# Gates, branch projections and feed forward computed token-major instead of channel-major

## The chip, the cores and the metric

The kernel runs on one core of one Trainium2 chip, in one launch. The metric is device time in microseconds, the median of several runs. Engines are named as the profile names them: PE (TensorE matmul), PEld (its weight load), DVE (VectorE), ACT (ScalarE), POOL (GpSimd), SP (which issues DMAs here).

## The reference

Two blocks, each two layers deep, run on `x` of 256 tokens by 1024 channels in float32. The first block is a mixer of three groups of 512 channels (block attention, HGRN2, memory attention); the second has a mixer (delta rule, retention, pooling) and a SwiGLU feed forward of 2816 hidden channels. What the change touches:

```
# first block, per layer; z has 3 x 512 channels
y = jnp.concatenate([o_a, o_h, o_m], axis=-1) * jax.nn.silu(z)
x = x + y @ w_out[l]

# second block, mixer, per layer; gates have 3 x 1024 channels
o_dn  = (rms-normalised o_dn) * dn_out_norm * jax.nn.silu(dn_z)
o_ret = (normalised o_ret) * ret_out_norm * jax.nn.silu(ret_g)
gt = jax.nn.sigmoid(gates).reshape(b, s, N_BRANCH, D_MODEL)
y = (gt[:, :, 0] * (o_dn @ w_branch_dn) + gt[:, :, 1] * (o_pool @ w_branch_pool)
     + gt[:, :, 2] * (o_ret @ w_branch_ret))
return y @ w_out

def swiglu(h, w_gate, w_up, w_down):
    return (jax.nn.silu(h @ w_gate) * (h @ w_up)) @ w_down
```

## The kernel before

**Products in three parts.** A float32 product is made of three matmuls on rounded operands: high by high, high by low, low by high. Activations lie transposed (channels on partitions) in `aTh` and `aTl`, 512 channels by 256 tokens each. Weights come as units of 256 x 512 numbers (512 KB): a DMA into `raw` (three buffers), a cast on ACT to the high part `wh`, a subtraction on DVE to the low part `wl`. Class `Stream` (L224) does this ahead of use, with six slots for split units and two spare ones for some of them; a slot is free when the last matmul of its unit has been issued. SP's queue issues the loads in the order of use.

**Two ways to run a projection.** `tok` (L545) is token-major: for each of the two tiles of 128 tokens, the activations are the stationary operand and 512 weight columns move; the result `acc` has tokens on partitions. It takes a unit in the first token tile and frees it in the second. `chan` (L566) is channel-major: 128 weight columns are stationary and the 256 tokens move; the result has channels on partitions, which is the layout that a next contraction wants. With four column blocks it takes its units in a first pass over two blocks and frees them in a second; in the feed forward (two blocks) it takes and frees a unit at once.

**Where each is used.** Channel-major before: f and q of the first block (`hgrn_f`, L826), the three z (L850), k, q and v of the delta branch with their convolution (L1568), `dn_z` and `ret_g` (L1588), the six gates (L1594), the six branch products (L1599), and gate and up of the feed forward from its third tile of 256 hidden channels on (L1681). Token-major: the other projections, and the first 512 hidden channels. `gated` (L632) turns a branch's output with four 128 x 128 transposes on PE (`to_T`, L425) and multiplies by the silu of z. `ffn` (L1658) does the down projection of tile j - 2 after gate and up of tile j; `hid` holds the hidden channels as high and low parts `ff`.

**What sets the order.** Work is written as generators that yield what they wait for. `Order` (L146) keeps an estimate of PE's time and of when each tile is ready, and after every few matmuls (`poll`) it issues the steps whose inputs it takes to be ready within 200 ns. So the place of a transpose in PE's queue follows from an estimate; on the chip each engine takes its queue in order and waits for its inputs by semaphores. PSUM has three `acc` banks and five `mx` banks; in the feed forward four `mx` banks hold the down projection's sums.

Of the kernel before, what the change touches and what calls it, by code (L numbers as in the profile page):

```python
# [20 lines left out]
NT = 2  # L21
# [5 lines left out]
NJ = D_FF // 256  # L27
NEG = -1.0e30
# [7 lines left out]
SKEW, FSKEW, URGENT = 3, 3, 4  # L36
# [187 lines left out]
class Stream:  # L224
# [15 lines left out]
    def _dma(self):  # L240
        i = self.n_dma
        ap = self.units[i][1]
        _, kk, n = ap.shape
        t = self.kb.p_raw.tile([P, 1024], F32, tag="raw", name=f"raw{i}")
        self.kb.nc.sync.dma_start(t[:, : kk * n].rearrange("p (k n) -> p k n", k=kk), ap)
# [3 lines left out]
        self.n_dma += 1  # L249

# [7 lines left out]
    def _split_h(self):  # L258
# [10 lines left out]
        w = math.prod(self.units[i][1].shape[1:])  # L269
# [3 lines left out]
    def _split_l(self):  # L273
        i = self.n_l
        w = math.prod(self.units[i][1].shape[1:])
# [17 lines left out]
    def take(self, key):  # L293
# [11 lines left out]
        _, kk, n = self.units[i][1].shape  # L305
# [13 lines left out]
def rows(ap, r0, c0, kk, n):  # L319

    return ap[r0 : r0 + kk * P, c0 : c0 + n].rearrange("(k p) n -> p k n", p=P)


class Kernel:
# [92 lines left out]

    def copy(self, dst, src):
# [38 lines left out]
    def silu(self, out, x, gain=None):  # L457

        yield x
        zc, s = self.k2([P, 2, S], "zc"), self.k2([P, 2, S], "sg")  # L460
# [3 lines left out]
        if gain is None:  # L464
            self.dve.tensor_tensor(out, zc, s, op=ALU.mult)
        else:
            for j in range(2):
                self.dve.scalar_tensor_tensor(out[:, j, :], zc[:, j, :], gain[j], s[:, j, :], op0=ALU.mult, op1=ALU.mult)
# [5 lines left out]
    def halves(self, x):  # L474
        return [x[:, 512 * i : 512 * i + 512] for i in range(2)]
# [69 lines left out]
    def tok(self, hT, keys, evac, own=True):  # L545


        w = {}
        for t in range(NT):
            if own:  # L550
                self.join_hT(t)
            for key in keys:
                ps = self.acc()
                for u in range(KD // 2):
                    if t == 0:
                        w[key, u] = self.stream.take((key, u))
                    for k in range(2):
                        kk = 2 * u + k
                        self.mm3(ps, tuple(x[:, kk % 4, t * P : (t + 1) * P] for x in hT[kk // 4]),
                                 tuple(x[:, k, :] for x in w[key, u]), kk == 0, kk == KD - 1)  # L560
# [5 lines left out]
    def chan(self, hT, key, evac, nu=KD // 2, ku=2, nj=4, own=True):  # L566

        if own:
            self.join_hT(0, 1)
# [62 lines left out]
    def gated(self, o, sz, oT, t, needs):  # L632

        yield needs
        ts = slice(t * P, (t + 1) * P)
        on = o()
        yield on
        tp = self.to_T(on)
        yield [tp] + list(sz)
        y = self.k2([P, 4, P], "y")  # L640
        for j in range(2):
            self.dve.tensor_tensor(y[:, 2 * j : 2 * j + 2, :], tp[:, 2 * j : 2 * j + 2, :], sz[j][:, :, ts], op=ALU.mult)
        yield y
        d = (slice(None), slice(None), ts)
        yield from self.split(oT[0][d], oT[1][d], y)
        yield oT[1]
# [166 lines left out]
    def layer1(self, l, hT, mem, nxt):  # L813
# [33 lines left out]
        for br in (1, 0, 2):  # L847
            gain = [ogain[:, 0:1]] * 2 if br == 1 else None
            sz = [self.k2([P, 2, S], "sz") for _ in range(2)]
            self.chan(hT, (l, f"z{br}"), lambda j, ps: self.silu(sz[j], ps, gain))  # L850
            oT[br] = self.part()
            for t in range(NT):
                o.spawn(self.gated(lambda key=(br, t): on[key], sz, oT[br], t, [f"on{l}{br}{t}"]), f"oT{l}{br}{t}")
# [273 lines left out]
    def units2(self, l):  # L1127
# [22 lines left out]
        for n in ("gate", "up"):  # L1150
            cols("f" + n, a[f"ffn_{n}_2"][l], 0, spare=True)

        def down(j, i, spare):
            u.append((((l, "fdown", j), i), rows(a["ffn_down_2"][l], 256 * j, 512 * i, 2, 512), spare))

        for j in range(2, NJ):
            for n in ("gate", "up"):
                for i in range(2):
                    u.append((((l, "f" + n, j), i), rows(a[f"ffn_{n}_2"][l], 512 * i, 256 * j, 4, 256), False))
            if j - 2 < NJ - FSKEW:  # L1160
                for i in range(2):
                    down(j - 2, i, False)
        for j, i in self.last_downs():
            down(j, i, True)
        return u

    def last_downs(self):
        return [(j, i) for i in range(2) for j in range(NJ - FSKEW, NJ - 1)] + [(NJ - 1, i) for i in range(2)]
# [35 lines left out]
    def retention(self, l, qT, kT, rv, on):  # L1204
# [15 lines left out]
        yield [f"rv{l}0", f"rv{l}1"]  # L1220
        yield [R0, R1, rv]
        for t in range(NT):
# [6 lines left out]
            self.o.spawn(self.ret_norm(t, ps, on), f"on{l}ret{t}")  # L1229

    def ret_norm(self, t, ps, on):
# [9 lines left out]
        dve.tensor_tensor(o, o, self.bc(r), op=ALU.mult)  # L1241
# [287 lines left out]
    def gate_evac(self, sg, ps):  # L1529
        yield ps  # L1530
        z = self.k2([P, 2, S], "gz")
# [3 lines left out]
    def branch_evac(self, br, c, j, ps, sg, y, yT):  # L1535
# [7 lines left out]
        if br == "dn":  # L1543
            d = (slice(None), slice(2 * j, 2 * j + 2), slice(None))
            yield y
            yield from self.split(yT[c][0][d], yT[c][1][d], y)
            yield yT[c][1]

    def mixer2(self, l, hT, nxt):
# [6 lines left out]
        self.load(lay[:, 52:56], a["ret_out_norm_2"][l].rearrange("(n p) -> p n", p=P))  # L1556
# [29 lines left out]
        for br, n, gain in (("dn", "dn_z", [lay[:, 48:49]] * 4), ("ret", "ret_g", [lay[:, 52 + j : 53 + j] for j in range(4)])):  # L1586
            sz[br] = [self.k2([P, 2, S], "sz") for _ in range(2)]
            self.chan(hT, (l, n), lambda j, ps: self.silu(sz[br][j], ps, gain[2 * j : 2 * j + 2]))  # L1588
        y = [[self.k2([P, 2, S], "y") for _ in range(2)] for _ in range(2)]
        yT = []  # L1590

        def gate(br, c):
            sig = [self.k2([P, 2, S], "sig") for _ in range(2)]
            self.chan(hT, (l, ("g", br, c)), lambda j, ps: self.gate_evac(sig[j], ps))  # L1594
            return sig

        def branch(br, c, sig):
            o.join(*([f"oT{l}pool"] if br == "pool" else [f"oT{l}{br}{t}" for t in range(NT)]))
            self.chan([oT[br]], (l, ("b", br, c)),  # L1599
                      lambda j, ps: self.named(f"y{l}{br}{c}{j}", self.branch_evac(br, c, j, ps, sig[j], y[c][j], yT)),  # L1600
                      nu=2, own=False)

        for br, _ in self.B2_GATES:
            if br != "pool":
                oT[br] = self.part()
                for t in range(NT):
                    o.spawn(self.gated(lambda key=(br, t): on[key], sz[br], oT[br], t, [f"on{l}{br}{t}"]), f"oT{l}{br}{t}")
# [10 lines left out]
        for c in range(2):  # L1618
            for j in range(2):
                for t in range(NT):  # L1620
                    o.spawn(self.named_wait(f"y{l}dn{c}{j}"), f"yT{l}{c}{j}{t}")
        self.out_proj([(yT[p], (l, "wo2", p), [f"yT{l}{p}0", f"yT{l}{p}1"]) for p in range(2)], SKEW,
# [10 lines left out]
    def ff_first(self, gate, key, t, ps, f, hid):  # L1633

        if gate:
            yield from self.silu(f.rearrange("p (a b) -> p a b", a=2), ps.rearrange("p (a b) -> p a b", a=2))
            return
# [3 lines left out]
        tp = self.to_T(f)  # L1641
        ts = slice(t * P, (t + 1) * P)
        yield tp
        for j in range(2):
            self.act.copy(hid[j][:, 0, :, ts], tp[:, 2 * j : 2 * j + 2, :])
        for j in range(2):
            yield hid[j]
            self.dve.tensor_tensor(hid[j][:, 1, :, ts], tp[:, 2 * j : 2 * j + 2, :], hid[j][:, 0, :, ts].bitcast(F32), op=ALU.subtract)
        yield hid[1]

    def ff_up(self, ps, f, hid):
        yield [ps, f]
        self.dve.tensor_tensor(f, ps, f, op=ALU.mult)
        yield f
        yield from self.split(hid[:, 0], hid[:, 1], f)
        yield hid

    def ffn(self, l, hT, nxt):  # L1658
        a, o = self.a, self.o
        hid = {j: self.k4([P, 2, 2, S], "ff", F32R) for j in range(2)}  # L1660
        f1 = [self.k2([P, 512], "f") for t in range(NT)]
        self.tok(hT, [(l, "fgate"), (l, "fup")],
                 lambda key, t, ps: self.named(f"ff{l}{key[1]}{t}", self.ff_first(key[1] == "fgate", key, t, ps, f1[t], hid)))
# [4 lines left out]
        def down(j, t, i):  # L1668
            o.join(*([f"ff{l}fup{t}" for t in range(NT)] if j < 2 else [f"ff{l}{j}"]))
# [8 lines left out]
        for j in range(2, NJ):  # L1678
            f = self.k2([P, 2, S], "f")
            hid[j] = self.k4([P, 2, 2, S], "ff", F32R)  # L1680
            self.chan(hT, (l, "fgate", j), lambda _, ps: self.silu(f, ps), nu=2, ku=4, nj=2)  # L1681
            self.chan(hT, (l, "fup", j), lambda _, ps: self.named(f"ff{l}{j}", self.ff_up(ps, f, hid[j])), nu=2, ku=4, nj=2)
            if j - 2 < NJ - FSKEW:
                for t in range(NT):
                    for i in range(2):
                        down(j - 2, t, i)
# [117 lines left out]
```

## Time and profile before

| what | value |
|---|---|
| median of 3 runs | 1437.85 us (1437.79 to 1439.17) |
| profiled execution | 1441.07 us, span 1439.3 us |
| mean granted TensorE clock | 0.996 |
| PE busy | 1403.6 us (98%), 9772 matmuls |
| DVE busy | 1024.6 us (71%) |
| ACT busy | 831.5 us (58%) |
| read from HBM | 228.76 MB |

The span runs from the first to the last instruction of the profiled execution; its time also has what lies around them. Matmuls are pipelined, so the records of one and the next overlap, and a busy PE is not one at its peak: how far apart matmuls begin tells more than how long each lasts.

### The profile page before, as it was taken

To read this page: it belongs to the slowest core of one execution; us is meant where nothing else is said; L and a number is where in the kernel's file an instruction comes from. 1 tells how busy PE (TensorE), PEld (TensorE's weight loads), DVE (VectorE), ACT (ScalarE), POOL (GpSimd) and SP (SyncE) were. 2 spreads that over 40 slices of the span, in tenths; PEclk is the share of its full clock that TensorE was granted. 3 is DMA by queue.
4 is the path that set the end of the run, shared out by engine and by line. 5 is a ranking of instruction groups with operands and counts; after the bars stand their busy time and mean duration, and the time that the engine had idled before them with its cause. 6 is when DMAs were issued, how large, how long until landed. Compare 5 with 4: busy or idle time off the path is not lost.

```text
span 1439.3 us, 24675 instructions
## 1 busy us (share of the span) xinstructions
PE 1403.6 (98%) x9772; PEld 1285.8 (89%) x9772; DVE 1024.6 (71%) x1684; ACT 831.5 (58%) x1396; POOL 24.0 (2%) x65
## 2 busy tenths in 40 slices
PE   6899999999998999999999999999999999999998
PEld 6778998888997899999988999979899999799997
DVE  5887778598777698585677656687976577765554
ACT  5875666586665476554655545556655456554553
POOL 6000000000000000000000000000000000000000
PEclk9999999999999999999999999999999999999999
DMA  8752455554256464253475666645543355566662
GB/s 273 173 163 75 132 206 177 185 164 118 60 188 228 126 186 126 90 162 97 156 235 166 186 188 189 215 136 156 153 135 109 105 154 204 184 190 190 184 183 88
DMA packets 156564, 231.41 MB, mean 161 GB/s; under 512 B 27168, under 2 KB 65696, under 8 KB 156448
## 3 DMA queue, kind: packets, MB, share of 16 engines
q1 hardware_dynamic: 156416, 229.84, 52.5%
q8 instruction: 76, 1.25, 0.4%
q14 instruction: 40, 0.33, 0.1%
q0 software_dynamic: 32, 0.00, 0.0%
HBM read 228.76 MB, written 1.05 MB: 160 GB/s over the span
## 4 chain that ended last, share of the span: by engine, by line
PE 76%; DMA 9%; DVE 8%; ACT 4%; issue 2%; SPq 0%; DVEq 0%; ACTq 0%
PE acc L134 53%; PE mx L134 19%; DVE wl L108 4%; PE mx L142 4%; DMA raw<-in_w_in 3%; DMA raw<-in_w_out 3%; ACT wh L108 3%; DMA raw<-in_ffn_up 1%; DMA raw<-in_w_mem_kv 1%; DVE aTl L108 1%; DMA raw<-in_ffn_down 0%; DVE x L108 0%; DMA gain<-in_norm_g 0%; ACT hE L108 0%; ACT junk L108 0%
## 5 line engine op out<-in xcount | busy, mean ns | idle before, releaser
L108 DVE TENSOR_TENSOR wl<-raw,wh 128x1024 fp32r<-128x1024 f32 x412 | 502.2, 1223 | 209.7 <-ACT wh L108 205.9
L108 ACT CAST wh<-raw 128x1024 fp32r<-128x1024 f32 x412 | 429.6, 1048 | 317.7 <-PE acc L134 148.7
L134 PE MATMUL acc<-aTh,wh 128*128 128x256 f32 x1792 | 514.1, 287 | 0.0
L134 PE MATMUL acc<-aTh,wl 128*128 128x256 f32 x1792 | 508.3, 284 | 0.6 <-DVE wl L108 0.6
L134 PE MATMUL acc<-aTl,wh 128*128 128x256 f32 x1792 | 507.6, 283 | 0.0
L134 PEld LDWEIGHTS acc<-aTh,wl 128*128 128x128 f32 x1792 | 343.5, 192 | 2.4 <-DVE wl L108 0.8
L134 PEld LDWEIGHTS acc<-aTh,wh 128*128 128x128 f32 x1792 | 343.4, 192 | 1.9 <-issue 0.5
L134 PEld LDWEIGHTS acc<-aTl,wh 128*128 128x128 f32 x1792 | 343.3, 192 | 0.0
L134 PE MATMUL acc<-wh,aTh 128*128 128x512 f32 x496 | 201.0, 406 | 6.0 <-ACT aTh L108 4.7
L134 PE MATMUL acc<-wh,aTl 128*128 128x512 f32 x496 | 195.4, 395 | 0.8 <-DVE aTl L108 0.8
L134 PE MATMUL acc<-wl,aTh 128*128 128x512 f32 x496 | 195.8, 395 | 0.0
L134 PEld LDWEIGHTS acc<-wh,aTh 128*128 128x128 f32 x496 | 94.4, 190 | 26.3 <-ACT aTh L108 5.8
L134 PEld LDWEIGHTS acc<-wh,aTl 128*128 128x128 f32 x496 | 93.9, 189 | 21.9 <-DVE aTl L108 2.3
L134 PE MATMUL mx<-wh,ff 128*128 128x512 f32 x352 | 111.6, 390 | 0.0
L134 PEld LDWEIGHTS acc<-wl,aTh 128*128 128x128 f32 x496 | 94.2, 190 | 18.4 <-issue 0.5
L134 PEld LDWEIGHTS mx<-wh,ff 128*128 128x128 f32 x352 | 66.2, 188 | 13.4
L108 ACT ACTIVATE sg<-sg 128x512 f32<-128x512 f32 x116 | 73.1, 630 | 1.9
L134 PE MATMUL mx<-wl,ff 128*128 128x512 f32 x176 | 68.7, 390 | 0.0
L108 ACT ACTIVATE sg<-zc 128x512 f32<-128x512 f32 x58 | 36.5, 628 | 22.8 <-DVE zc L108 22.8
L108 ACT ACTIVATE sig<-gz 128x512 f32<-128x512 f32 x24 | 15.2, 632 | 57.8 <-DVE gz L108 57.8
L134 PEld LDWEIGHTS mx<-wl,ff 128*128 128x128 f32 x176 | 33.1, 188 | 6.2
L108 DVE TENSOR_SCALAR zc<-acc 128x512 f32<-128x512 f32 x46 | 31.6, 686 | 9.5 <-PE acc L134 9.5
(311 smaller groups left out, 1593.0 us busy)
## 6 DMA issues: line engine op xcount, KB each, us to landing
raw<-in_w_in SPq DMA_DIRECT2D x200, 512.0 KB, 4.2
raw<-in_ffn_gate SPq DMA_DIRECT2D x44, 512.0 KB, 3.9
raw<-in_ffn_up SPq DMA_DIRECT2D x44, 512.0 KB, 4.6
raw<-in_ffn_down SPq DMA_DIRECT2D x44, 512.0 KB, 4.2
raw<-in_w_out SPq DMA_DIRECT2D x40, 512.0 KB, 3.8
raw<-in_w_mem_kv SPq DMA_DIRECT2D x16, 512.0 KB, 4.2
raw<-in_w_branch_pool SPq DMA_DIRECT2D x8, 512.0 KB, 3.7
raw<-in_w_branch_ret SPq DMA_DIRECT2D x8, 512.0 KB, 4.5
```

What stands on the lines that cost most here:

```text
L108: r = f(out, *args, **kw)
L134: self._ns.matmul(out, lhsT, rhs, **kw)
L142: self._ns.transpose(out, x, ident)
```

## The change

All the projections named above as channel-major, except f, q and the delta branch's k, q and v, go through `tok`. Their results have tokens on partitions. `turn` is new: it transposes a token-major product and splits it into the high and low parts; a gain per channel is applied there. It serves `gated` (which now multiplies first and turns the product) and the delta branch's sum `y` ahead of the output projection. In the feed forward gate and up run by chunks of 512 hidden channels (a last one has 256 columns of either in one unit, `flast`), and each chunk's product is turned with four transposes per token tile; the down projection of chunk c - 1 follows gate and up of chunk c. The gain of the retention's norm varies along the free axis now and is loaded as a broadcast tile. `cols`, `rows` and `Stream` are adapted to units that come from two loads.

```
+    def turn(self, x, oT, t, gain=None):
+        yield x
+        d = (slice(None), slice(None), slice(t * P, (t + 1) * P))
+        tp = self.to_T(x)
+        yield tp
+        if gain is None:
+            self.act.copy(oT[0][d], tp)
+        else:
+            self.act.activation(oT[0][d], tp, AF.Copy, scale=gain)
+        yield oT[0]
+        if gain is None:
+            self.dve.tensor_tensor(oT[1][d], tp, oT[0][d].bitcast(F32), op=ALU.subtract)
...
     def gated(...)
-        tp = self.to_T(on)
-        yield [tp] + list(sz)
-        y = self.k2([P, 4, P], "y")
-        for j in range(2):
-            self.dve.tensor_tensor(y[:, 2 * j : 2 * j + 2, :], tp[:, 2 * j : 2 * j + 2, :], sz[j][:, :, ts], op=ALU.mult)
-        yield y
-        yield from self.split(oT[0][d], oT[1][d], y)
+        yield [on, sz[t]]
+        y = self.k2([P, G], "y")
+        self.dve.tensor_tensor(y, on, sz[t], op=ALU.mult)
+        yield from self.turn(y, oT, t, gain)
...
-            self.chan(hT, (l, f"z{br}"), lambda j, ps: self.silu(sz[j], ps, gain))
+            self.tok(hT, [(l, f"z{br}")], lambda key, t, ps: self.silu(sz[t], ps))
...
     def units2(...)
+        for c in range(NC):
+            cols(("fgate", c), wg, 512 * c, spare=c == 0)
+            cols(("fup", c), wu, 512 * c, spare=c == 0)
+            if c:
+                down(c - 1)
...
     def ret_norm(...)
-        dve.tensor_tensor(o, o, self.bc(r), op=ALU.mult)
+        for h in range(4):
+            dve.scalar_tensor_tensor(o[:, h, :], o[:, h, :], r[:, h : h + 1], gain[:, h * P : (h + 1) * P],
+                                     op0=ALU.mult, op1=ALU.mult)
...
     def branch_evac(...)
         if br == "dn":
-            yield from self.split(yT[c][0][d], yT[c][1][d], y)
+            yield from self.turn(y, yT[c], t)
...
     def mixer2(...)
-            self.chan(hT, (l, n), lambda j, ps: self.silu(sz[br][j], ps, gain[2 * j : 2 * j + 2]))
+            self.tok(hT, [(l, n)], lambda key, t, ps: self.silu(sz[br][t], ps))
...
-            self.chan(hT, (l, ("g", br, c)), lambda j, ps: self.gate_evac(sig[j], ps))
+            self.tok(hT, [(l, ("g", br, c))], lambda key, t, ps: self.gate_evac(sig[t], ps))
...
-            self.chan([oT[br]], (l, ("b", br, c)),
+            self.tok([oT[br]], [(l, ("b", br, c))],
...
     def ff_up(...)
         self.dve.tensor_tensor(f, ps, f, op=ALU.mult)
         yield f
-        yield from self.split(hid[:, 0], hid[:, 1], f)
+        n = 2 * len(hid)
+        tp = self.to_T(f, n)
+        yield tp
+        for j, x in enumerate(hid):
+            self.act.copy(x[:, 0, :, ts], tp[:, 2 * j : 2 * j + 2, :])
+        for j, x in enumerate(hid):
+            yield x
+            self.dve.tensor_tensor(x[:, 1, :, ts], tp[:, 2 * j : 2 * j + 2, :], x[:, 0, :, ts].bitcast(F32), op=ALU.subtract)
...
     def ffn(...)
-        for j in range(2, NJ):
-            self.chan(hT, (l, "fgate", j), lambda _, ps: self.silu(f, ps), nu=2, ku=4, nj=2)
-            self.chan(hT, (l, "fup", j), lambda _, ps: self.named(f"ff{l}{j}", self.ff_up(ps, f, hid[j])), nu=2, ku=4, nj=2)
+        for c in range(NC + 1):
+            keys = [(l, (n, c)) for n in (("fgate", "fup") if c < NC else ("flast",))]
+            for ks in ([keys] if c == 0 else [[k] for k in keys]):
+                self.tok(hT, ks, evac)
```

On PE, in the feed forward of the second block's first layer, the end of an up projection and the start of the down projection behind it, before. `acc` is the up projection's sum, `mx` with `ff` the down projection's.

```order
L134 MATMUL acc_9038<-aTh_8416,wl_8928 128x256
L134 MATMUL acc_9038<-aTl_8417,wh_8927 128x256
L134 MATMUL mx_8780<-wh_8954,ff_8522 128x512
L134 MATMUL mx_8780<-wl_8955,ff_8522 128x512
L134 MATMUL mx_8780<-wh_8954,ff_8522 128x512 x2
L134 MATMUL mx_8780<-wl_8955,ff_8522 128x512
L134 MATMUL mx_8780<-wh_8954,ff_8522 128x512
L134 MATMUL mx_8781<-wh_8968,ff_8522 128x512
```

The same place now, chunk 2, second token tile; `ident,f` are the four transposes of that tile's product.

```order
L135 MATMUL acc_8365<-wl_8302,aTh_7603 128x512
L135 MATMUL acc_8365<-wh_8301,aTl_7604 128x512
L135 MATMUL mx_7710<-wh_8314,ff_7973 128x512
L135 MATMUL mx_7710<-wl_8315,ff_7973 128x512
L135 MATMUL mx_7710<-wh_8314,ff_7973 128x512 x2
L135 MATMUL mx_7710<-wl_8315,ff_7973 128x512
L135 MATMUL mx_7710<-wh_8314,ff_7973 128x512
L135 MATMUL mx_7711<-wh_8345,ff_7973 128x512
L135 MATMUL mx_7711<-wl_8346,ff_7973 128x512
L143 MATMUL mx_8427<-ident_92,f_8242 128x128 x4
```

The operands have changed sides and sizes, and a group of transposes stands eight matmuls into the down projection.

On DVE, the same tile's steps before, from the silu's product with the up projection on (`f`), with the weight splits `wl` around them.

```order
L108 TENSOR_TENSOR wl_9067<-raw_8985,wh_9066 128x1024
L108 TENSOR_TENSOR f_8966<-acc_9038,f_8966 128x512
L108 TENSOR_TENSOR wl_9098<-raw_9015,wh_9097 128x1024
L108 TENSOR_TENSOR ff_8967<-f_8966,ff_8967 128x512
L108 TENSOR_TENSOR wl_9125<-raw_9052,wh_9124 128x1024
```

And now, for the second token tile of chunk 2.

```order
L109 TENSOR_TENSOR wl_8395<-raw_8334,wh_8394 128x1024
L109 TENSOR_TENSOR wl_8409<-raw_8362,wh_8408 128x1024
L109 TENSOR_TENSOR f_8242<-acc_8365,f_8242 128x512
L109 TENSOR_TENSOR wl_8425<-raw_8389,wh_8424 128x1024
L109 TENSOR_TENSOR ff_8243<-mx_8427,ff_8243 128x2x128
L109 TENSOR_TENSOR ff_8244<-mx_8427,ff_8244 128x2x128
```

`f` stands behind two splits in a row, and the low part of the hidden channels is made out of PSUM in two halves.

## Rows read from the trace of the kernel before

**Rows 1.** The page: busy time by engine; granted clock in tenths, 40 slices.

```profile
PE 1403.6 (98%) x9772; PEld 1285.8 (89%) x9772; DVE 1024.6 (71%) x1684; ACT 831.5 (58%) x1396; POOL 24.0 (2%) x65
...
PEclk9999999999999999999999999999999999999999
```

**Rows 2.** The page: the chain that ended last, by engine.

```profile
PE 76%; DMA 9%; DVE 8%; ACT 4%; issue 2%; SPq 0%; DVEq 0%; ACTq 0%
```

**Rows 3.** The chain of waits in order of time: start, us, what, matmul count.

```profile
795.05 5.47 PE mx L134 x24
800.52 11.51 PE acc L134 x96
...
951.27 8.24 PE acc L134 x35
...
1184.57 37.29 PE acc L134 x300
...
1416.38 16.36 PE mx L134 x72
```

**Rows 4.** Busy time by stretch: feed forward, then gates and branches.

```profile
800.00:930.00 130.00, 130.00 (x933) 123.22 (x932) 76.92 (x77) 66.24 (x78) 0.00 (x0) 1.00 0.64 193
650.00:718.00 68.00, 68.00 (x572) 67.50 (x571) 40.41 (x58) 36.94 (x54) 0.00 (x0) 1.00 0.41 125
```

**Rows 5.** Instruction groups by shape on PE: busy us, mean ns, idle before.

```profile
L134 PE MATMUL acc<-aTh,wh 128*128 128x256 f32 x1792 | 514.1, 287 | 0.0
...
L134 PE MATMUL acc<-wh,aTh 128*128 128x512 f32 x496 | 201.0, 406 | 6.0 <-ACT aTh L108 4.7 <-DVE x L108 1.3
L134 PE MATMUL acc<-wl,aTh 128*128 128x512 f32 x496 | 195.8, 395 | 0.0
```

**Rows 6.** Timeline of PE: start us, us, instruction; two groups of transposes.

```profile
768.09 0.60 PE L142 MATMUL mx<-ident,xn 128*128 128x128 f32 x4
768.44 0.48 PE L134 MATMUL acc<-wh,aTh 128*128 128x512 f32 x1
...
773.09 0.66 PE L142 MATMUL mx<-ident,f 128*128 128x128 f32 x4
773.50 0.47 PE L134 MATMUL acc<-wh,aTh 128*128 128x512 f32 x1
```

**Rows 7.** Timeline of all engines round a group that waits.

```profile
782.92 1.23 DVE L108 TENSOR_TENSOR wl<-raw,wh 128x1024 fp32r<-128x1024 f32 x1 [0.64 <-ACT wh L108]
...
784.07 0.68 DVE L108 TENSOR_TENSOR f<-acc,f 128x512 f32<-128x512 f32 x1
...
784.24 0.28 PE L134 MATMUL acc<-aTh,wh 128*128 128x256 f32 x1
...
784.81 0.66 PE L142 MATMUL mx<-ident,f 128*128 128x128 f32 x4 [0.29 <-DVE f L108]
```

**Rows 8.** The chain of waits at the start of the feed forward.

```profile
750.30 3.68 DMA raw<-in_ffn_up
...
778.19 3.58 DMA raw<-in_ffn_down
...
781.84 1.05 ACT wh L108
```

**Rows 9.** Waits by engine and releaser on PE: us, times, longest.

```profile
PE mx L142 <- DVE xn L108: 16.9, 7, 10.4
...
PE mx L142 <- DVE f L108: 0.6, 2, 0.3
```

**Rows 10.** Instructions on tile `ff`: ns min/median/max, first and last start us, shape.

```profile
L108 ACT CAST ff<-f x18: 611/612/622, 796.0 to 1417.5; 128x512 fp32r<-128x512 f32 x18
L108 DVE TENSOR_TENSOR ff<-f,ff x18: 684/686/692, 797.3 to 1418.2; 128x512 fp32r<-128x512 f32 x18
L108 ACT CAST ff<-mx x8: 372/376/383, 773.8 to 1271.3; 128x256 fp32r<-128x256 f32 x8
L108 DVE TENSOR_TENSOR ff<-mx,ff x8: 413/416/418, 774.8 to 1272.5; 128x256 fp32r<-128x256 f32 x8
```

More of the change, by code (lines that the diff above doesn't have):

```diff
@@ L27 @@
 NJ = D_FF // 256
+NC = D_FF // 512
 NEG = -1.0e30
@@ L249, in _dma, with shape @@
         self.n_dma += 1
+    def shape(self, i):
+        aps = self.units[i][1]
+        return P, aps[0].shape[1], sum(ap.shape[2] for ap in aps)
     def _can_place(self):
@@ L274, in _split_l @@
         i = self.n_l
-        w = math.prod(self.units[i][1].shape[1:])
+        w = math.prod(self.shape(i)[1:])
         h = self.h[i][:, :w]
@@ L304, in take @@
         self.at += 1
-        _, kk, n = self.units[i][1].shape
+        _, kk, n = self.shape(i)
         self.o.pe = max(self.o.pe, self.o.ready[self.l[i].name])
@@ L455, in sigmoid, with silu @@
         self.act.activation(s, s, AF.Exp, scale=-1.0)
-    def silu(self, out, x, gain=None):
+    def silu(self, out, x):
         yield x
-        zc, s = self.k2([P, 2, S], "zc"), self.k2([P, 2, S], "sg")
+        zc, s = self.k2(x.shape, "zc"), self.k2(x.shape, "sg")
         self.dve.tensor_scalar(zc, x, -43.0, None, op0=ALU.max)
@@ L463, in silu @@
         yield s
[L464 to L468 removed]
+        self.dve.tensor_tensor(out, zc, s, op=ALU.mult)
     def evac(self, dst, ps):
@@ L472, in evac, with halves @@
         self.copy(dst, ps)
-    def halves(self, x):
-        return [x[:, 512 * i : 512 * i + 512] for i in range(2)]
+    def halves(self, x, n=512):
+        return [x[:, n * i : n * i + n] for i in range(2)]
     def norm(self, x, gb, hT, t, ss=None):
@@ L551, in tok @@
                 self.join_hT(t)
+            if wait:
+                self.o.join(f"{wait}{t}")
             for key in keys:
                 ps = self.acc()
-                for u in range(KD // 2):
+                for u in range(nu):
                     if t == 0:
@@ L1220, in retention @@
         yield [f"rv{l}0", f"rv{l}1"]
+        gain = self.load(self.k2([P, G], "retg"), self.a["ret_out_norm_2"][l].unsqueeze(0).to_broadcast([P, G]))
         yield [R0, R1, rv]
@@ L1617, in mixer2 @@
         gp = self.gain(a["mix_post_norm_2"][l])
[L1618 to L1622, printed above, removed]
+        self.out_proj([(yT[p], (l, "wo2", p), [f"y{l}dn{p}"]) for p in range(2)], SKEW,
                       lambda t, ps: o.spawn(self.post_norm(t, ps, gp, nxt(t)), f"h{self.ph + 1}{t}", True))
@@ L1630, in named, with ff_up @@
         self.o.done.add(name)
[L1633 to L1637, printed above, removed]
+    def ff_up(self, ps, f, t, hid):
         yield [ps, f]
@@ L1668, in down @@
         def down(j, t, i):
-            o.join(*([f"ff{l}fup{t}" for t in range(NT)] if j < 2 else [f"ff{l}{j}"]))
+            o.join(f"ff{l}{j // 2}{t}")
             if t == 0:
@@ L1676, in down, with evac @@
                 self.stream.free()
-        for j in range(2, NJ):
-            f = self.k2([P, 2, S], "f")
-            hid[j] = self.k4([P, 2, 2, S], "ff", F32R)
-            self.chan(hT, (l, "fgate", j), lambda _, ps: self.silu(f, ps), nu=2, ku=4, nj=2)
-            self.chan(hT, (l, "fup", j), lambda _, ps: self.named(f"ff{l}{j}", self.ff_up(ps, f, hid[j])), nu=2, ku=4, nj=2)
[L1683 to L1686, printed above, removed]
+        def evac(key, t, ps):
+            n, c = key[1]
+            js = [j for j in (2 * c, 2 * c + 1) if j < NJ]
+            hs = [hid[j] for j in js]
+            if n == "fgate":
+                return self.silu(f[t], ps)
+            if n == "fup":
+                return self.named(f"ff{l}{c}{t}", self.ff_up(ps, f[t], t, hs))
+            h = self.halves(ps, S)
+            return self.named(f"ff{l}{c}{t}", self.chain(self.silu(f[t][:, :S], h[0]), self.ff_up(h[1], f[t][:, :S], t, hs)))
+        for c in range(NC + 1):
+            f = [self.k2([P, 512], "f") for _ in range(NT)]
+            for j in range(2 * c, min(2 * c + 2, NJ)):
+                hid[j] = self.k4([P, 2, 2, S], "ff", F32R)
+            keys = [(l, (n, c)) for n in (("fgate", "fup") if c < NC else ("flast",))]
+            for ks in ([keys] if c == 0 else [[k] for k in keys]):
+                self.tok(hT, ks, evac)
+            if 0 < c < NC:
+                for j in (2 * c - 2, 2 * c - 1):
+                    for t in range(NT):
+                        for i in range(2):
+                            down(j, t, i)
         nxt(None)
```

109 lines of the change are left out of this document (46 added, 63 removed).

## The prediction

> **What bounds the kernel now.** I read the page's busy shares first, then the chain of waits, then single stretches. The reader should see in [rows 1] that PE works 98% of the span at a granted clock that shows 9 in all 40 slices (90% or more of full, so the upper of its two levels, 2.4 GHz), while DVE has 71% and ACT 58%; in [rows 2] that the chain that ended last lies on PE for 76%, on DMA, DVE and ACT for 21%. So PE's instruction stream is the bound, apart from the starts of stages. [Rows 3] shows it piece by piece: from 795 us on, the feed forward is an unbroken run of 96 channel-major matmuls (11.51 us) and 24 for the down projection (5.47 us), and in the mixer's gates 300 matmuls take 37.29 us with nothing between. In [rows 4] DVE is busy 76.92 of 130 us and ACT 66.24 in the feed forward, 40.41 and 36.94 of 68 in the gates: both have room. What counts is what PE issues and how far apart.
>
> The profiled execution took 1441.07 us with a span of 1439.3; the median of the runs is 1437.85, 3.2 lower. I sum changes against the profiled execution and take the sum from the median.
>
> **The matmuls converted.** [Rows 5]: 3 x 1792 = 5376 matmuls move 256 token columns (three such rows in the view, the first is shown). The order of the changed kernel keeps 960 of them (f, q of the first block; k, q, v of the delta branch). The other 4416 become 2208 that move 512 weight columns; the columns are the same, the count is halved. The durations of [rows 5] (287 and 406 ns) overlap with the next matmul and cannot be multiplied; the spacing can be read from the unbroken runs of [rows 3]: 11.51/96 = 0.1199 us for 256 columns; for 512, 5.47/24 = 0.2279, 16.36/72 = 0.2272. I take 0.2275. Removed: 4416 x 0.1199 = 529.5 us. Added: 2208 x 0.2275 = 502.3. Term: -27.2 us. Ends: at 0.2272, -27.9; at 8.24/35 = 0.2354, the 512-column run at a mixer's start, where weights come late, -9.7. I hold to 0.2275 because the converted stretches are the full runs of [rows 3], not a stage's start.
>
> The Trainium skill ("TensorE: Matmul & The Clock Gate", in the part on the 56 ns gap) gives start to start N/2.4 + 2.5 ns at 2.4 GHz, 109.2 and 215.8 ns here. By that rule the halved count would give back only 4416 x 0.1092 - 2208 x 0.2158 = 5.7 us, an estimate from the page. The trace does not agree: 119.9 and 227.5 ns, about 13 ns over the column time at either size, and it decides.
>
> **The transposes added.** A token-major result must be turned before it can be contracted again. The order holds 700 transposes of this kind where it held 596: per layer 4 groups of 4 for the mixer's output and 8 groups of 4 plus 2 of 2 more in the feed forward; 24 groups of 4 and 4 of 2 in all. The gates' products were turned before too (earlier, ahead of the product), so they add none. [Rows 6]: a group holds PE from 768.09 to 768.44, 0.35 us, or from 773.09 to 773.50, 0.41. Taking 0.38 and half of it, 24 x 0.38 + 4 x 0.2 = 9.9 us; ends 9.2 and 10.6. All of it lies on PE, so it counts. Term: +9.9.
>
> **The waits added.** PE takes its queue in order, so a transpose that is placed before DVE has its input holds up the matmuls behind it. 48 groups now stand right behind a DVE product: 20 new in the feed forward, 8 for the mixer's output, 20 of the gates that moved behind the product with z. Before shows both ends in the same form: in [rows 6] the group at 773.09 starts on time; in [rows 7] the one at 784.81 waits, because a weight split (`wl`, 1.23 us from 782.92, itself behind a late DMA, [rows 8]) stands ahead of `f` on DVE: the matmul before starts at 784.24, so 0.57 us to the group against 0.12 usual, 0.45 lost. In the new order the t = 1 group of a feed forward chunk stands 8 matmuls, 1.82 us, behind the end of its up projection, with two splits ahead of `f` on DVE; the t = 0 group stands 9 matmuls, 2.05 us, behind with none directly ahead. The later of the two splits needs the slot of the third up unit, which ends 1.36 us before that projection does. From there: 0.17 us until the matmul's result is out (0.395 long at a spacing of 0.2275, [rows 5]), cast 1.05 [rows 8], split 1.23 and product 0.68 [rows 7], some 0.1 between them: 3.23 - 1.36 = 1.87 us behind the projection's end, 0.05 late, and later if the DMA is. So I charge 8 new t = 1 groups 0.3 us (between 0.1 and 0.45) and the other 40 about 0.02: [rows 9] shows 0.6 us over two waits for `f`, and no line at all for the products kn, dnqn or ry, which also stand right behind DVE. Term: +3.2 us; ends 0 and 48 x 0.45 = 21.6. Behind a waiting group stand the matmuls that free weight slots, so ACT's next cast waits with it; that is why I do not expect recovery.
>
> **What lies beside other work.** ACT and DVE turn the hidden layer out of PSUM in two halves of 256 ([rows 10]: 2 x 376 ns for 612 on ACT, 2 x 416 for 686 on DVE), some 0.14 us a group on either, hidden by their idle share in [rows 4]; without that cover it would be 20 x 0.14 = 3 us. The retention's gain now costs four DVE instructions of 128 columns a tile for one of 512 (at most the 416 ns of 256 columns each, for 686, [rows 10]), under 1 us for each of four tiles, hidden by the gates' matmuls; its load is one more DMA on SP's queue per layer, ahead of later weights; a neighbour of it takes 3.6 us to land [rows 8], and three raw buffers cover that. The gain that went into z's product now goes into the copy out of PSUM, one instruction for one. The last chunk's three remaining downs cover its chain as before. In the feed forward the weights come in bursts of four now instead of evenly; the mixer's gates of [rows 3] take them in the same bursts at full rate.
>
> **Sum.** -27.2 + 9.9 + 3.2 = -14.1: 1441.1 becomes 1427, and the median 1437.85 - 14 = 1424 us. The feed forwards give little of it: 432 x 2 x 0.1199 - 432 x 0.2275 = 5.3 us a layer, less 3.4 for transposes and more for waits. The mixer gives 6.5 less 1.5 a layer, the first block 1.8 a layer, less where waits set the pace there.
>
> **Rivals.** (1) *The transposes wait.* Place: the 48 groups; price 0.45 us each; -27.2 + 9.9 + 21.6 = +4.3, 1442 us. It decides from 17.3/48 = 0.36 us a group. For it: the t = 1 group of [rows 7] is just of this form, and happens in both layers. Against it: most DVE-fed groups in [rows 9] lose nothing.
> (2) *The bursts starve PE in the feed forward.* 18 gate and up tiles follow each other in bursts of four units in 5.5 us; a unit needs DMA (3.6 us, [rows 8]), cast and split (2.3) behind three raw buffers. If each tile waits 1.5 us, +27: 1451 us; it turns the sign from 14/18 = 0.8 us a tile. For it: the first chunk of [rows 8] does wait for DMA. Against it: the gates in [rows 3].
> (3) *Halving the count gives back less.* At the spacing 0.2354 of the mixer's start, -9.7 + 9.9 + 3.2 = +3.4, 1441 us. Against it: two runs of [rows 3] at 0.227 to 0.228. The Trainium skill's rule above ("TensorE: Matmul & The Clock Gate", on the 56 ns gap) goes the same way and further, by its figures to -5.7 + 9.9 + 3.2 = +7.4, an estimate.
> (4) *No new wait and some old ones gone.* -27.9 + 9.2 = -18.7, and some of the 16.9 us for `xn` [rows 9] fall away in a new order: 1413 to 1418.
>
> **How the numbers follow.** Forecast (1419 to 1434): 0.62. (4): 0.12. (1), in part or whole: 0.12, a third of it still faster, a third within the bound. (2): 0.07. (3): 0.07, half within 0.2%. I count 0.2% (1435.0 to 1440.7) as what a measurement can tell from no change. Faster 0.62 + 0.12 + 0.04 = 0.78; same 0.04 + 0.04 and a little of (2) = 0.09; slower 0.13. The range 1412 to 1438 leaves out the larger part of (1) to (3).
>
> **What would show it.** Right: the feed forward's run per two hidden tiles falls from 2 x 16.98 us to 33.5 to 33.8; `acc` with 512 columns stays at 0.227; the mixer's gate run shortens by 5%; PE waits for `f` and `y` together under 6 us. Wrong: PE waiting for `f` or `y` over 15 us in total (1), PE or its weight loads waiting for `wl` or `wh` inside the feed forward (2), a spacing of 0.23 or more in unbroken runs (3). A time above 1438 makes the prediction wrong, one below 1412 too.

## The result, and the profile after

The changed kernel takes 1430.88 us (median of 5 runs, 1427.54 to 1434.69) where the one before takes 1437.85; the ratio is 0.9943, with an interval of 0.9924 to 0.9962. A second series (experiment 5) gave 1431.14 and 0.9947 [0.9928, 0.9967]. So it is faster, by some 7 us: the forecast of 1424 had the direction and the time lies in its range, but half of the 14 us is missing.

The page of the profiled execution (1427.61 us, span 1425.8), against [rows 1, 2]: busy time by engine, granted clock, chain by engine.

```profile
PE 1387.7 (97%) x7668; PEld 1173.1 (82%) x7668; DVE 1021.5 (72%) x1686; ACT 834.7 (59%) x1422; POOL 25.1 (2%) x65
...
PEclk9999999999999999999999999999999999999999
...
PE 78%; DMA 9%; DVE 7%; ACT 4%; issue 2%; SPq 0%; DVEq 0%; ACTq 0%
```

The picture is the same as before with fewer matmuls: PE is the bound. The profiled executions differ by 13.5 us, more than the medians: before's is one of its long ones (1441.07), after's one of its short ones. I measure terms in them, and hold sums against the medians.

The chain of waits, one chunk of 512 hidden channels in the feed forward and the start of the next (start, us, what, count), against the first two of [rows 3]:

```profile
798.14 9.08 PE mx L135 x40
807.22 18.37 PE acc L135 x81
825.59 0.44 PE mx L143 x4
826.03 3.41 PE acc L135 x15
829.44 1.81 PE mx L135 x8
831.25 0.49 PE mx L143 x4
831.74 9.10 PE mx L135 x40
```

From 798.14 to 831.74 it takes 33.60 us, where two tiles of 256 took 2 x 16.98 before: inside the 33.5 to 33.8 that the prediction named. In part that is luck: its matmuls were 0.12 us too dear (144 x 0.2275, where experiment 2 shows 32.64) and its two groups of transposes 0.20 too cheap. 18.37/81 is 0.2268 us a matmul, also as named. The mixer's gates, 300 matmuls in 37.29 us before (the last 12, from 1218.95 on, already have 512 columns, so 37.29/300 is no spacing), now show runs such as this one:

```profile
667.79 24.50 PE acc L135 x108
```

That is 0.2269 each, where 216 of the old ones at 0.1199 would be 25.90: 5% shorter. So the steady stretches do what was summed. What they leave out stands between the runs (in the first listing the two groups of transposes, 0.44 and 0.49 us), and at the ends of stages. There PE waits; the view of its waits (total, times, longest), against [rows 9]:

```profile
PE mx L143 <- DVE xn L109: 15.7, 6, 10.4
PE mx L143 <- DVE y L109: 4.0, 5, 2.1
...
PE mx L143 <- DVE f L109: 2.6, 5, 1.3
```

The line for `y` is new and the one for `f` has grown from 0.6. Since a record lasts longer than the distance to the next matmul, such idle time understates what is lost. I take instead, for each group, the time from the start of the matmul before it to its own start, less the 0.227 (0.120 behind a channel-major matmul) that is usual: 5.3 us ahead of the 28 groups on `y` and 3.4 ahead of the 24 on `f`, 8.7 in all; in the second series' profile 6.2 and 4.4, 10.6 in all; before, 0.9 on `f`. The eight second-tile groups of the middle chunks, which the prediction charged, lose nothing. Four groups have 5.5 of the 8.7: 2.23 at 430.50, 1.43 at 918.21, 1.00 at 1199.72 and 0.81 at 195.1, all near the end of a stage, ahead of an output projection or of the last down projections, for whose weights ACT waits there (0.48 to 3.32 us). The timeline round the first of them, DVE, ACT and PE (start, us, instruction, and in brackets the idle time before it and what ended it):

```profile
426.24 1.05 ACT L109 CAST wh<-raw 128x1024 fp32r<-128x1024 f32 x1 [1.46 <-DMA raw<-in_w_out]
...
427.32 1.23 DVE L109 TENSOR_TENSOR wl<-raw,wh 128x1024 fp32r<-128x1024 f32 x1 [2.46 <-ACT wh L109]
...
428.46 0.69 DVE L109 TENSOR_TENSOR sz<-zc,sg 128x512 f32<-128x512 f32 x1
...
429.67 0.68 DVE L109 TENSOR_TENSOR y<-on,sz 128x512 f32<-128x512 f32 x1
...
430.50 0.63 PE L143 MATMUL mx<-ident,y 128*128 128x128 f32 x4 [2.07 <-DVE y L109]
```

Read it from the top: a weight DMA is late, ACT waits 1.46 us for it, and DVE stands 2.46 us at `wl` with `sz` and `y` behind it in its queue; PE has the transposes of `y` next, and the matmuls behind them wait too. It is the form of [rows 7], at five times the price, and in the gates and the first block, to which the prediction gave 0.02 us a group.

A late weight alone does not do it. In the middle chunk above ACT waits 1.84 us for one, but `f` stands ahead of its split on DVE, and the transposes start on time:

```profile
830.35 0.68 DVE L109 TENSOR_TENSOR f<-acc,f 128x512 f32<-128x512 f32 x1
831.01 1.05 ACT L109 CAST wh<-raw 128x1024 fp32r<-128x1024 f32 x1 [1.84 <-DMA raw<-in_ffn_gate]
...
831.09 0.65 PE L143 MATMUL mx<-ident,f 128*128 128x128 f32 x4
```

It was so in the kernel before, with `ry` beside a weight that is 2.12 us late; PE has no wait for `ry` there:

```profile
488.34 1.05 ACT L108 CAST wh<-raw 128x1024 fp32r<-128x1024 f32 x1 [2.12 <-DMA raw<-in_w_in]
488.65 0.75 DVE L108 TENSOR_TENSOR ry<-ry,rz 128x256 f32<-128x256 f32 x2
489.42 1.23 DVE L108 TENSOR_TENSOR wl<-raw,wh 128x1024 fp32r<-128x1024 f32 x1
```

### The profile page after: what moved, and what is told of

Read it like the earlier page. It is cut to its first block, busy times and chain, and to the rows that moved or that the text cites. A ratio compares the mean times of both kernels' runs of the same rounds, so it can differ in the third digit from the quotient of the medians.

```text
span 1425.8 us, 20549 instructions
## 1 busy us (share of the span) xinstructions
PE 1387.7 (97%) x7668; PEld 1173.1 (82%) x7668; DVE 1021.5 (72%) x1686; ACT 834.7 (59%) x1422; POOL 25.1 (2%) x65
## 4 chain that ended last, share of the span: by engine, by line
PE 78%; DMA 9%; DVE 7%; ACT 4%; issue 2%; SPq 0%; DVEq 0%; ACTq 0%
PE acc L135 54%; PE mx L135 18%; PE mx L143 5%; DVE wl L109 4%; DMA raw<-in_w_in 3%; ACT wh L109 3%; DMA raw<-in_w_out 2%; DMA raw<-in_ffn_down 1%; DMA raw<-in_ffn_up 1%; DVE aTl L109 0%; DMA gain<-in_norm_g 0%; DMA mem<-in_mem 0%; DVE yg L109 0%; ACT sg L109 0%; DVE x L109 0%
## 5 line engine op out<-in xcount | busy, mean ns | idle before, releaser
L135 PE MATMUL acc<-wh,aTh 128*128 128x512 f32 x1232 | 495.7, 402 | 3.4 <-ACT aTh L109 3.4
L135 PE MATMUL acc<-wh,aTl 128*128 128x512 f32 x1232 | 483.0, 393 | 1.1 <-DVE aTl L109 1.1
L135 PE MATMUL acc<-wl,aTh 128*128 128x512 f32 x1232 | 483.2, 392 | 0.0
L135 PEld LDWEIGHTS acc<-wl,aTh 128*128 128x128 f32 x1232 | 232.0, 188 | 44.2 <-issue 1.0
L135 PE MATMUL acc<-aTh,wh 128*128 128x256 f32 x320 | 91.6, 286 | 0.0
L135 PE MATMUL acc<-aTl,wh 128*128 128x256 f32 x320 | 91.3, 285 | 0.0
L135 PE MATMUL acc<-aTh,wl 128*128 128x256 f32 x320 | 91.3, 285 | 0.0
L135 PEld LDWEIGHTS acc<-aTh,wh 128*128 128x128 f32 x320 | 62.1, 194 | 0.2
L135 PEld LDWEIGHTS acc<-aTh,wl 128*128 128x128 f32 x320 | 62.0, 194 | 0.2
L135 PEld LDWEIGHTS acc<-aTl,wh 128*128 128x128 f32 x320 | 62.1, 194 | 0.0
```

The source lines that it names most:

```text
L135: self._ns.matmul(out, lhsT, rhs, **kw)
```

## Experiments

**1. Feed forward back to channel-major, the rest as changed.**

```
-        for c in range(NC + 1): ... self.tok(hT, ks, evac)
+        for j in range(2, NJ): ... self.chan(hT, (l, "fgate", j), ..., nu=2, ku=4, nj=2)
```

> The feed forward goes back to channel-major as in the kernel before; gates and branch projections stay token-major. Theory A (the spacing gives what was summed, and the waits for products of VectorE take part of it back): the stage starts of the two traces give the feed forwards 2.1 and 1.3 us of the 13.5, so this kernel keeps 10 of the 13.5 in its profile: 0 to 4 us slower than the changed kernel, 1427 to 1434 us, ratio to before 0.992 to 0.997. PE's waits for f fall from 2.6 us to under 1.5, those for y stay near 4. Rival B (the gain follows the number of matmuls converted, and nothing else differs between the stages): the feed forward holds 1728 of the 4416, 39%, so 39% of the 7 to 10 us go: 1433 to 1436 us, ratio 0.997 to 0.999.

1432.81 us (1427.88 to 1435.29), ratio to before 0.9956 [0.9940, 0.9972]. The time lies in A's range and just below B's: the feed forward's conversion is worth 1 to 2 us (the intervals overlap; the prediction's terms: 5.3 less 3.4 less 1.2 a layer, 1.4 for both), the rest of the change about 6, where the prediction's terms give some 13. So most of the gap lies in the first block and the mixer, where this kernel's PE waits for `y` as in the changed one:

```profile
PE mx L143 <- DVE y L109: 5.0, 5, 2.2
...
PE mx L143 <- DVE f L109: 1.9, 2, 1.0
```

(Its `f`, two groups, I had expected under 1.5.)

**2. The feed forward's transposes left out.**

```
-        tp = self.to_T(f, n)
+        tp = f.rearrange("p (h d) -> p h d", h=n)
...
-        yield tp
```

(ACT and DVE then read `f` itself in place of PSUM.)

> The feed forward's 88 transposes are left out: the product f is copied as it is into the hidden layer's place (so the down projection contracts values that are not turned, and the output differs from the reference's). Theory A: 20 groups of 4 at 0.38 us and 4 of 2 at 0.2, 8.4 us, and the 3.4 us that PE lost ahead of these groups: 9 to 12 us below the changed kernel, 1417 to 1421 us, ratio to before 0.986 to 0.989. Rival B (PE is held by weights that come late in the feed forward, so the transposes stand in time that would be lost anyway): under 4 us below the changed kernel, ratio 0.991 or more, and the period of a chunk stays above 33 us.

1414.22 us (1411.18 to 1415.79), 0.9826 [0.9809, 0.9843]: 16.8 below the changed kernel, so A's direction and more than its 9 to 12. The chain shows where the more is, one chunk without transposes:

```profile
806.44 21.76 PE acc L135 x96
828.20 10.88 PE mx L135 x48
839.08 21.76 PE acc L135 x96
```

From 806.44 to 839.08 is 32.64 us, where the chunk with two groups took 33.60: 0.48 us a group, not the 0.38 that I took from [rows 6]. The timeline of PE in the changed kernel shows the rest of the price:

```profile
825.19 0.40 PE L135 MATMUL acc<-wh,aTl 128*128 128x512 f32 x1
825.42 0.60 PE L143 MATMUL mx<-ident,f 128*128 128x128 f32 x4
825.78 0.48 PE L135 MATMUL acc<-wh,aTh 128*128 128x512 f32 x1
826.10 0.39 PE L135 MATMUL acc<-wl,aTh 128*128 128x512 f32 x1
```

The next matmul starts 0.36 us after the group, but the one behind it only 0.32 later in place of 0.23, and its record lasts 0.48 instead of 0.39. The 0.48 and 0.47 stood in [rows 6] too, and I read only the starts. Twenty groups at 0.48, four half ones at half of that and the 3.4 to 4.4 us of waits for `f` make 14 to 15 of the 16.8; the rest is within the spread of the runs. B is out: in these chunks PE runs without a break.

**3. Transposes of `y` and `f` placed later in PE's queue** (also run with 3.0 us, experiment 7).

```
         yield x
+        yield self.o.ready[x.name] + 1500.0
         d = (slice(None), slice(None), slice(t * P, (t + 1) * P))
         tp = self.to_T(x)
```

and the same behind `yield f` in `ff_up`.

> The transposes behind the products y and f are put 1.5 us of planned TensorE time later in PE's queue, with other matmuls ahead of them; nothing else is changed. Theory A (PE loses 8.7 us at these groups because DVE's queue has late weight splits ahead of y and f): the loss ahead of them falls to under 4 us where there is other work to put ahead, and the time by 3 to 6 us against the changed kernel: 1422 to 1428 us, ratio to before 0.990 to 0.993. Rival B (the same late weights hold PE at the next matmul, so the wait only changes its name): PE waits for wh, wl or hid tiles instead, the time within 1.5 us of the changed kernel's, ratio 0.993 to 0.996.

1425.90 us (1423.68 to 1429.7), 0.9914 [0.9897, 0.9931]: 4 to 5 below the changed kernel. The waits for `f` fell from 2.6 to 0.2 us in the view; those for `y` did not fall:

```profile
PE mx L143 <- DVE y L109: 3.8, 4, 1.7
```

By starts, 0.4 us are lost ahead of `f` (from 3.4 to 4.4) and 4.9 ahead of `y` (from 5.3 to 6.2). So half of A: the time of the waits for `f` is won, that ahead of `y` is not with this lag (it is with 3.0, at another price: experiment 7).

**4. A fourth raw buffer.**

```
-    RAW, SLOTS, SPARE, AHEAD = 3, 6, 2, 6
+    RAW, SLOTS, SPARE, AHEAD = 4, 6, 2, 6
-K4, K2, SM, ACC = 12, 24, 24, 3
+K4, K2, SM, ACC = 12, 22, 24, 3
```

> A fourth raw buffer, so four weight units are under way at once in place of three; paid for with 22 in place of 24 small tiles. Theory A (a late weight DMA at a stage's end makes the cast and the split late, and these stand ahead of y and f on DVE): the groups at the stage ends lose half or less of their 8.7 us, the starts of stages a little too: 3 to 7 us below the changed kernel, 1421 to 1428 us, ratio to before 0.989 to 0.993. Rival B (the DMA queues' rate is the limit, or the two tiles that are missing cost as much): within 2 us of the changed kernel or slower, and the losses ahead of y and f stay above 7 us.

1432.63 us (1424.51 to 1438.39), 0.9955 [0.9935, 0.9975]: no gain, a miss for A. The loss ahead of `f` fell to 0.4, but `y` has 7.1 us, nearly all in three groups, and the starts of stages became worse:

```profile
PE mx L143 <- DVE xn L109: 19.5, 7, 10.2
PE mx L143 <- DVE y L109: 6.4, 3, 2.4
```

Whether the two missing tiles or the other order did that, one run cannot tell. Its runs spread by 14 us, and those with a lower mean clock are the longer: 1424.51 at 0.998, 1437.94 at 0.990. Its longest wait for `y`, in a table by stretch (us, busy times, then granted clock, DMA share, GB/s):

```profile
196.00:198.90 2.90, 0.99 (x5) 0.49 (x3) 1.44 (x2) 2.52 (x4) 0.00 (x0) 1.00 0.12 45
199.07:202.48 3.41, 3.05 (x10) 2.59 (x11) 3.41 (x5) 2.29 (x4) 0.00 (x0) 0.50 0.58 165
202.50:206.00 3.50, 3.50 (x17) 2.86 (x16) 2.02 (x3) 2.46 (x3) 0.00 (x0) 1.00 0.83 273
```

PE works 0.99 of 2.9 us, and then the clock is at half (1.2 GHz) for a stretch. There matmuls of 512 columns start 0.43 us apart, not 0.227, so a wait can cost twice:

```profile
201.17 0.63 PE L135 MATMUL acc<-wh,aTl 128*128 128x512 f32 x1
201.60 0.63 PE L135 MATMUL acc<-wh,aTh 128*128 128x512 f32 x1
202.03 0.61 PE L135 MATMUL acc<-wl,aTh 128*128 128x512 f32 x1
```

That prices the clock, as an estimate: 0.20 us for each matmul of 512 columns that starts at half clock, 0.09 for one of 256 (0.213 apart, not 0.120). In this run's profile it makes some 7 us, in the two of the changed kernel 1.4 and 1.6, in that of the kernel before 3.0.

**5. The changed kernel again.**

> The changed kernel once more, with nothing edited, on the chip of the three kernels below and beside the kernel before. Theory A (the sum holds, waits ahead of y and f take 8 to 9 us, and stretches of about 3.4 or 6.8 us at half the granted clock that follow stalls of PE differ from execution to execution): 1427 to 1435 us, ratio 0.992 to 0.997; executions with a lower mean clock are the longer ones, 1.4 us of span for each 0.001 of clock or more; the profiled one loses 8 to 9 us ahead of y and f whatever its clock. Rival B (the spread between executions comes from weight DMAs that land at other times, and the clock has nothing to do with it): the spread stays where the clock is the same.

1431.14 us (1424.29 to 1434.42), 0.9947 [0.9928, 0.9967]. Loss ahead of `y` and `f` in the profile: 10.6 us, a little over the 8 to 9 expected. Over both series the runs go with the clock: 1424.29 at 0.999, 1427.54 and 1427.61 at 0.998, 1430.24 to 1434.69 for the seven at 0.997 and 0.996, 1433.88 at 0.995. Those of the kernel before, 62 in all with a clock on record, are at 0.998 in the middle, these at 0.997. A holds on the spread.

**6. A plan that knows when raw buffers come free, on the changed kernel, with the lag, and on the kernel before.**

```
-        self.dma_at = max(self.dma_at, self.o.pe) + self.DMA_NS
+        free = self.raw_free[i - self.RAW] if i >= self.RAW else 0.0
+        self.dma_at = max(self.dma_at, self.o.pe, free) + self.DMA_NS
```

(`raw_free` notes when each split is planned to end.)

> The plan that orders the queues is told that a weight DMA starts only when its raw buffer is free (after the split three units earlier), where before it counted the DMA from the time it is put in the queue; only the order changes, no instruction is added or removed. Theory A (a late wh and wl stand ahead of y, f or their inputs in DVE's in-order queue): splits move behind the products on DVE, the loss ahead of y and f falls below 5 us, the time by 2 to 6 us against the changed kernel. Rival B (the product chain itself is late, so what stands beside it on DVE does not matter): the loss stays at 8 to 9 us and the time within 1.5 us.

1434.09 us (1431.49 to 1435.67), 0.9967 [0.9954, 0.9980], 3 slower than the changed kernel beside it. The loss ahead of `y` fell to 1.7 and of `f` to 3.1, 4.8 in all as A had it, but the time did not follow. The new order lets PE stand at the starts of stages:

```profile
PE mx L143 <- DVE xn L109: 20.5, 7, 10.2
```

At the longest of them after the kernel's first a late split stands ahead of `xn` on DVE:

```profile
745.03 1.23 DVE L109 TENSOR_TENSOR wl<-raw,wh 128x1024 fp32r<-128x1024 f32 x1 [1.51 <-ACT wh L109]
...
746.96 1.41 DVE L109 SCALAR_TENSOR_TENSOR xn<-x,r,gain 128x512 f32<-128x512 f32 x2
...
747.85 1.51 PE L143 MATMUL mx<-ident,xn 128*128 128x128 f32 x6 [4.34 <-DVE xn L109]
```

So there the edit of the order put a late split ahead of `xn`; neither theory had that. The clock is as large a part: all six runs are at 0.991 to 0.994 (the changed kernel's at 0.995 to 0.999), and by the estimate of experiment 4 half clock costs some 7 us in this profile, over 5 more than in the changed kernel's.

> Both edits: the plan knows when raw buffers come free, and the transposes behind y and f stand 1.5 us of planned time later in PE's queue. Theory A: the loss ahead of y and f under 3 us, 6 to 9 us below the changed kernel, 1420 to 1426 us, ratio to before 0.987 to 0.992. Rival B (the two edits take away the same waits): no better than the lag alone, 1424 to 1428 us, ratio 0.990 to 0.993.

1422.92 us (1421.35 to 1425.41), 0.9894 [0.9879, 0.9908]: 8 below the changed kernel, in A's range. The loss ahead of `y` is 1.2, ahead of `xn` 4.1 (6.9 in the changed kernel); 3.6 of what is left is one group on `f`, the last of the first feed forward.

> The kernel before, with only the plan's rule on raw buffers changed (a weight DMA counts from the time its buffer is free). It has 4 transposes behind f and none behind y. Theory A (the rule helps by taking late splits from ahead of the products that PE waits for): little to gain here, since PE lost 0.9 us at such groups, so within 3 us of before, ratio 0.998 to 1.002, or slower where the starts of stages get their weights later, as the changed kernel did with this edit alone (PE lost 14 to 15 us ahead of xn, 9 before the edit). Rival B (the rule by itself is what makes the version with both edits faster than the changed kernel): 5 us or more below before, ratio under 0.997.

1443.05 us (1442.07 to 1444.6), 1.0026 [1.0010, 1.0042]: slower, as A allowed, with 19.5 us of waits for `xn` (16.9 before) and all six runs at a clock of 0.991 to 0.994. The rule alone helps neither kernel.

**7. The longer lag, with the rule and without.**

> Both edits as before, with a lag of 3.0 us in place of 1.5. Theory A (what is left is one wait of 3.6 us ahead of the last f of the first feed forward, and 1.1 us ahead of y): the wait ahead of f shortens by 1.5 us at least, 0 to 3 us below the version with 1.5, 1419 to 1423 us, ratio to before 0.987 to 0.990. Rival B (a longer lag only makes the hidden layer's parts late for the down projections, and PE waits there): the time 0 to 4 us above it, 1423 to 1427 us, ratio 0.990 to 0.992, with PE waiting for ff or aT tiles.

1422.23 us (1419.02 to 1423.55), 0.9888 [0.9873, 0.9903], the fastest of all that still transpose `f`: by the ratios 16 us below the kernel before and 8 below the changed one; not told apart from the lag of 1.5. Its profile has no line for `y`, and PE's waits for what is turned are these:

```profile
PE mx L143 <- DVE xn L109: 12.9, 7, 10.4
...
PE mx L143 <- DVE f L109: 0.8, 1, 0.8
```

With 1.0 us lost ahead of `y` and `f` and the upper clock up to the last matmul, the profiled execution takes 1419.02 (span 1417.2), just above the 1413 to 1418 of the prediction's rival (4), no new wait and some old ones gone; the median is 4 above it.

> The lag of 3.0 us alone, without the plan's rule on raw buffers. Theory A (the transposes' place behind the products is what costs; the rule only moves splits about, and alone made both kernels slower): as good as with the rule, 1419 to 1424 us, ratio to before 0.987 to 0.990, and PE loses under 2 us ahead of y and f. Rival B (y is held by the splits in DVE's queue, and only the rule takes them away): the loss ahead of y stays at 4 to 5 us as with 1.5 us, 1424 to 1427 us, ratio 0.990 to 0.993.

1436.02 us (1433.79 to 1438.09), 0.9986 [0.9975, 0.9998]: a miss for both. The loss ahead of `y` and `f` is 1.3 us, as A said, and yet it is 10 slower than with 1.5. The wait comes back behind the output projection:

```profile
PE mx L143 <- DVE xn L109: 22.6, 6, 10.2
...
PE mx L135 <- ACT aTh L109: 3.4, 2, 1.7
```

`y` turned later makes `aTh` late for the output projection, and at the two starts of the feed forward, 749.1 and 1237.6, PE loses 5.2 us each ahead of `xn`. The clock adds to it: all twelve runs are at 0.990 to 0.993 (0.996 to 0.998 with the lag of 1.5), by the estimate of experiment 4 some 8 us in this profile against 1.6. Why the rule on raw buffers takes all that away is not shown.

**8. Zeros for PE to multiply at the starts of stages.**

```
+            if late and b == 0:
+                fill = self.mx()
+                for _ in range(8):
+                    self.pe.matmul(fill, self.zero_bf, self.zero_bf.unsqueeze(1).to_broadcast([P, 4, P]), start=True, stop=True)
             tp.append(self.to_T(xn[b]))
```

`late` marks the first token tile of a norm of `x` behind an output or down projection.

> Eight bfloat16 matmuls of zeros, 512 columns each, are put in PE's queue in front of the first transposes of xn at each of the five stage starts behind an output or down projection, into a PSUM tile that nobody reads. Theory A (half-clock stretches follow stalls of PE; at these places they stop when PE does not stand still): 8 x 0.22 x 5 = 8.7 us of matmuls, of which 3 to 6 us lie in time that PE lost there anyway, so 3 to 5 us are added; against that no half-clock stretch begins at the stage starts at 222, 455, 747, 938 and 1229 us, which gives back 0 to 4 us: ratio to the changed kernel 0.999 to 1.003, mean clock 0.998 or more in most executions, and a spread under 5 us. Rival B (half-clock stretches come at times of their own): they still begin at these starts in some executions, the mean clock stays at 0.996 to 0.998 and the time is 5 us above the changed kernel.

1438.51 us (1436.35 to 1441.97), 1.0001 [0.9990, 1.0013]: 7 above the changed kernel, worse than either theory. The filling ahead of the transposes did not take PE's wait away; PE then stood behind them:

```profile
PE acc L135 <- ACT aTh L109: 6.4, 3, 2.3
```

Only four of the five fills stand at the starts that were meant. The wait at 224.23, 3.1 us, is for the memory's `xn`, which the edit does not touch (the first fill stands at 252.3), and half clock began 1.1 us behind it, at 225.31. At the filled starts it began at 754.38 and 948.93, in the new waits of 2.2 us, and not at the other two. In all three places half clock came in or behind a wait of PE, which speaks against B's account, though the time is B's; that it stops when PE does not stand still was not tested, since PE still stood.

## Why the prediction was right, and where its size was off

| term | predicted, us | as the runs show it, us |
|---|---|---|
| 4416 matmuls of 256 columns to 2208 of 512 | -27.2 | -29.0 (4416 x 0.1199 - 2208 x 21.76/96) |
| 104 transposes | +9.9 | +12.5 (24 groups at 0.48, four at half) |
| waits ahead of `y` and `f` | +3.2 | +7.8 to +9.7 (8.7 and 10.6, less 0.9 before) |
| sum | -14.1 | -8.7 to -6.8; medians -7.0 and -7.5 |

That the sum meets the medians within 2 us is more than it can promise: waits outside the table moved by as much (by the view `xn` -1.2 and -0.8 us, `hZ` +1.1 and +1.4, `aTh` -1.3 and -2.3).

- **The matmuls.** Right, and the spacing is the firmest part: 0.2267 to 0.2269 us in the unbroken runs shown of two kernels. Rival (3) is out; so is the rule of the Trainium skill weighed there ("TensorE: Matmul & The Clock Gate", the part on the 56 ns gap), which would put 215.8 ns where 226.7 are measured.
- **The transposes.** A mis-sized term: its upper end was 10.6. A group costs 0.48, of which some 0.09 is paid by the second matmul behind it (experiment 2).
- **The waits.** The step that failed, in place and size. I charged the steady t = 1 groups of the feed forward 0.3 us each, and they lose nothing; I charged all others 0.02, and a handful of them, at stage ends, lose up to 2.2. The evidence offered was that `kn`, `dnqn` and `ry` never wait. One `ry` is made right beside a late weight and is spared, with the split behind it (the result section); so what they showed is where the splits stood, not that a product of DVE is safe. [Rows 7] had the right mechanism, a late DMA and its split ahead of the product, and [rows 8] the late DMAs; what I did not ask was which products of the new order would stand behind such a split. It is rival (1) in small: about 0.2 us a group over 48, of which 0.36 would have turned the sign. The sign "under 6 us of waits for `f` and `y`" fell between: 6.6 and 8.3 by the view.
- **The bursts.** Rival (2) is out for the middle chunks: the 32.64 us without transposes are 144 matmuls at 0.2267 and nothing else.
- **Hidden work.** DVE and ACT have a point more than they had (72% and 59%), and the run of the gates is unbroken. That the smaller terms were hidden fits this; no run takes one away.
- **The clock.** Not in the prediction: the changed kernel has a slightly lower mean clock, with stretches at half clock behind its waits. As an estimate, 0.001 of mean clock is 2.9 us more at half clock, and at 1.4 to 1.6 us lost in a stretch of 3.4 (experiment 4) some 1.2 us of the medians' difference. The profile before has such a stretch too, from 755.56 to 762.39, where the 40 slices of [rows 1] all show 9. Why the weights are late at just these places is not shown.

## What to carry to other kernels

Before a result is turned on PE, ask what stands ahead of it in the queue of the engine that makes it: behind a step that waits for a late weight, the result is late too, and the sum over "usually hidden" groups misses it. Price an instruction by the period of a loop with and without it, not by its record: part of it may be paid by a later one. And a wait removed by order alone often comes back at the next join (experiments 6 and 7), so hold the time, not the wait, against the forecast; and look at the granted clock of every run, since a new wait can bring a stretch at half clock with it.

## What the runs showed of the hardware

A group of four 128 x 128 transposes between matmuls of 512 columns costs 0.48 us: they start 0.109 apart, the next matmul follows the last by 0.03, and the one after that comes 0.09 late.

The granted clock fell to half (1.2 GHz) in 12 of 13 profiled executions, 32 times ahead of the last matmul, each time in a wait of PE of over 1 us or within 2 us of its end, and rose again while PE worked. Many such waits had no fall behind them. At half clock matmuls of 512 columns start 0.427 us apart, those of 256 0.213, against 0.227 and 0.120. So two executions of one kernel can differ by some us though they run the same instructions in the same order.
